# Feed-forward of a decoder trunk: plain token blocks copied beside the mixed ones, and four parts instead of three

## Chip, cores and metric

The kernel runs on one core of one Trainium2 chip. The time is device microseconds of one launch, from the first to the last thing that the core does; lower is better. A result is the median of several executions.

## What is computed

The reference is a trunk of two layers on 256 tokens of 2048 features, in fp32: a gated DeltaNet mixer, a SwiGLU feed-forward, an HGRN2 mixer, a second SwiGLU feed-forward, with an RMSNorm ahead of each and one at the end. The change touches the two feed-forwards alone:

```python
D_MODEL, SEQ = 2048, 256
D_FF = -(-8 * D_MODEL // (3 * 256)) * 256          # 5632
def swiglu(h, w_gate, w_up, w_down):
    return (jax.nn.silu(h @ w_gate) * (h @ w_up)) @ w_down
...
    h = h + swiglu(rmsnorm(h, ffn_norm[layer]), ffn_w_gate[layer], ffn_w_up[layer], ffn_w_down[layer])
```

## The kernel before, in words

**Products.** Every matrix product is made in fp32 precision from three products in a rounded format: a weight tile `raw` (128x1024, 512 KB) is loaded, ScalarE (ACT) rounds it to `wh`, VectorE (DVE) subtracts to get the rest `wl`, and TensorE (PE) adds token-high by `wh`, token-high by `wl` and token-low by `wh`. The tokens' halves `xt_h`, `xt_l` (four tiles each, 256 tokens by 4x128 features) live in a constant pool. In `mm_rows` (line 666) the token tile of 128x128 is the stationary operand and 512 weight columns move. One *item* is one 128x1024 weight tile: twelve products of 512 columns. Items are a list, made once in Python; `stream` (line 629) keeps the loads and splits three items ahead (`AHEAD`, line 35), with four buffers each for `raw`, `wh` and `wl`.

**Groups and pairs.** The 5632 hidden features are 22 groups of 256 gate and 256 up columns. A *plain* group (`gate_up`, line 914) is 8 items; its end applies SiLU on ACT (`sg`) and the product with `up` on DVE (`h`), in `gated` (line 873). Two groups make a pair. A pair's result has to be turned to be the stationary operand of the down product, `hth` and `htl`. `turned` (898) does that through DRAM (`turn_through`, 818): four transposes inside 32x32 blocks on DVE, one DMA out and four in, on the queue of GpSimd (POOL). The pairs of `FF_QUICK` (line 34), and these alone, are turned on DVE without DRAM, half a pair (one group) at a time, by sixteen small transposes (`turn`, 808, `turned_half`, 907).

**Strassen groups.** 8 of the 22 groups in each feed-forward (four pairs) are made by `mixed_group` (934): the tokens in two halves, the features in two halves and gate and up as the two column halves give seven block products instead of eight, each with 256 moving columns. A group is 16 items: four rounds of four. In a round, item 1 makes product 1, item 2 products 2 and 3, item 3 products 5 and 7, item 4 products 6 and 4. Items 1 and 2 load weights (`sraw`), the weights of items 3 and 4 are sums on DVE. Products 3, 5, 6, 7 have mixed tokens as stationary operand, made at the phase's start by `mix_inputs` (832) into two tiles, `mixh` and `mixl`, that start at bytes 108 and 364 of a partition modulo 512 (offset 19 words, padding `PAD`). Products 1, 2, 4 read plain tokens from `xt_h` and `xt_l`. The seven products lie in four PSUM banks of the pool `aux`; plain and down items use two tiles of the pool `main`. At a group's end (`end`, 1007) ACT copies products 1 and 4 out, DVE makes the sums, and `gated` follows.

**Order.** `among` (512) spreads the Strassen items evenly behind plain or down items, all but the last `tail` ones. `FF_PLAN` (26) is in pairs: pair 0 plain, pair 1 by Strassen among pairs 2 and 3; pair 4 by Strassen among the first down part, pair 7 among 5 and 6; pair 8 among the second down part, then pairs 9 and 10 plain, then the third down part alone. A down part (`down`, 1043) multiplies the pairs of its part by the down weights, in four column groups `cg`; each loads the residual `x` from DRAM, adds the product (`add_x`) and stores it back. The last part's column groups also make the next phase's tokens (`next_input`) or the final norm (`finish`). The items' order on PE is fixed by this list.

**Planner.** All operations are recorded, and `plan` (314) simulates the engines with a table of costs and puts each engine's instructions in an order: among those that are ready, the one with the earliest due time (`late`) goes first. A due time is counted back from the item that needs the result; the serial length of several operations on one engine is not in it. The chip then runs each engine's list in that order, whatever the real times are.

Of the kernel before, what the change touches and what calls it, by code (L numbers as in the profile page):

```python
# [8 lines left out]
F32 = mybir.dt.float32  # L9
F32R = mybir.dt.float32r  # L10
U8 = mybir.dt.uint8
AF = mybir.ActivationFunctionType
# [5 lines left out]
P = 128  # L18
T = 256
# [2 lines left out]
CH = 64  # L22
N_HG = 8
N_FF = 22
FF_PARTS = (8, 8, 6)
FF_PLAN = (
    "0 | 1:2,3",
    "4:down | 7:5,6",
    "8:down | 9 | 10",
)  # L30
N_HGRN = 4
LEVELS = (64, 32, 16, 8, 4, 2, 1)
MASKED = LEVELS[2:]
FF_QUICK = (3, 6, 10)
AHEAD = 3
RAW_BUFS = 4
SPLIT_BUFS = 4
# [42 lines left out]


PAD = 64
IN_COLS = {"wh": 108, "wl": 364}


# [435 lines left out]


class Trunk:
# [294 lines left out]
    def turn_through(self, out, x):  # L818

        blocks = self.tile(self.pool, [P, 4, T], "blocks", bufs=1)  # L820
# [6 lines left out]
        self.nc.gpsimd.dma_start(home, blocks)  # L827
        home = home.rearrange("(a f) b r -> b f a r", a=4)
        for b in range(4):
            self.nc.gpsimd.dma_start(out[32 * b : 32 * b + 32], home[b])  # L830

    def mix_inputs(self):
# [6 lines left out]
        self.mixed = [[], [], [], []]  # L839
        both = [self.tile(self.pool, [P, 4096 + PAD], f"mix{x}", F32R)[:, 19 : 19 + 4096] for x in "hl"]  # L840
        row = self.rstd_row.unsqueeze(1).broadcast_to([P, 4, T])
        for q in range(2):
            uv = []
            for cg in (q, 2 + q):
                t = self.tile(self.pool, [P, 4, T], "turned", bufs=2, ordered=True)
                tt(t, self.xt_h[cg].bitcast(F32), self.xt_l[cg].bitcast(F32), ALU.add)
                tt(t, t, row, ALU.mult)
                uv += [t[:, :, 0:P], t[:, :, P:T]]
            a11, a21, a12, a22 = uv
            sums = []  # L850
            for _ in range(2):
                t = self.tile(self.pool, [P, 2, 512], "h1", bufs=2, ordered=True)
                sums += [t[:, i, :].rearrange("p (k t) -> p k t", k=4) for i in range(2)]
            s1, s2, s3, s4 = sums
            tt(s1, a21, a22, ALU.subtract)
            tt(s2, a11, s1, ALU.subtract)
            tt(s3, a21, a11, ALU.subtract)
            tt(s4, a12, s2, ALU.subtract)
            for n in range(4):
                h, low = (  # L860
                    m[:, (2 * n + q) * 512 : (2 * n + q + 1) * 512].rearrange("p (k t) -> p k t", k=4)
                    for m in both
                )
                nc.scalar.activation(h, sums[n], AF.Copy)
                tt(low, sums[n], h.bitcast(F32), ALU.subtract)
                self.mixed[n].append((h, low))

    def ffn(self, j, after):
        nc, a = self.nc, self.a
        hts, h1s, quick = {}, {}, {}  # L870
        gu = a[f"ffn_gu{j}"]

        def gated(gi, tt, gate, up, col):
# [3 lines left out]
            out = h1s[gi // 2][:, tt, gi % 2 * T : (gi % 2 + 1) * T]  # L877
            sg = self.tile(self.pool, [P, T], "sg", bufs=2)
# [17 lines left out]
            )  # L896

        def turned(pair):
            t = self.tile(self.pool, [P, 4, T], "turned", bufs=2, ordered=True)
            self.turn_through(t, h1s[pair])  # L900
            places(pair)
            split(
                pair, t.rearrange("p a (m s) -> p m a s", s=32),
                lambda x: x.rearrange("p n (t a s) -> p (n t) a s", t=2, s=32),
            )

        def turned_half(gi):
            pair, half = divmod(gi, 2)
# [7 lines left out]
        def gate_up(gi):  # L916
            def end(ps):
                for tt in range(2):
                    gated(gi, tt, ps[:, tt, 0:T], ps[:, tt, T:512], self.rstd[:, tt : tt + 1])
                if gi // 2 in FF_QUICK:  # L920
                    turned_half(gi)
                elif gi % 2:
                    turned(gi // 2)
# [6 lines left out]
        def mixed_pair(pair):  # L930

            return mixed_group(2 * pair) + mixed_group(2 * pair + 1, lambda: turned(pair))

        def mixed_group(gi, then=None):

            banks, raws = [], {}
            tok = slice(0, P), slice(P, T)

            def plain(k0, tt):
                def operand(kt):  # L940
                    cg = k0 + kt // 4
                    return self.xt_h[cg][:, kt % 4, tok[tt]], self.xt_l[cg][:, kt % 4, tok[tt]]
                return operand

            def mixed(n):
                def operand(kt):
# [60 lines left out]
            def end():  # L1007
                t = lambda n, tag: self.tile(self.pool, [P, n], tag, ordered=True)
                first, last = self.rstd[:, 0:1], self.rstd[:, 1:2]
                p1, p4, v, c11 = t(T, "p1"), t(T, "p4"), t(T, "p6"), t(T, "p2")  # L1010
                both = t(2 * T, "p37").rearrange("p (h c) -> p h c", h=2)
                w = both[:, 0]
# [5 lines left out]
                nc.vector.tensor_tensor(out=v, in0=product(6), in1=p1, op=ALU.subtract)  # L1018
                nc.vector.tensor_tensor(out=p1, in0=product(5), in1=v, op=ALU.add)
                nc.vector.tensor_tensor(  # L1020
                    out=both, in0=banks[1].rearrange("p (h c) -> p h c", h=2),
                    in1=p1.unsqueeze(1).broadcast_to([P, 2, T]), op=ALU.add,
                )
                nc.vector.tensor_tensor(out=v, in0=product(7), in1=v, op=ALU.add)
                nc.vector.tensor_tensor(out=p4, in0=p4, in1=v, op=ALU.subtract)
                gated(gi, 0, c11, both[:, 0], None)
                gated(gi, 1, p4, both[:, 1], None)
                if then:
                    then()

            items = []
            for kk in range(4):
# [36 lines left out]

        items, waiting = [], None  # L1070
        for part, steps in enumerate(FF_PLAN):
            order = []
            for step in steps.split(" | "):
                mix, _, beside = step.partition(":")
                if not beside:
                    order.append(int(step))
                    items += gate_up(2 * order[-1]) + gate_up(2 * order[-1] + 1)
                    continue
                many = []
                if beside == "down":  # L1080
                    many, waiting = waiting, None
                else:
                    for p in beside.split(","):
                        order.append(int(p))
                        many += gate_up(2 * order[-1]) + gate_up(2 * order[-1] + 1)
                order.insert(-1 if beside != "down" else 0, int(mix))
# [774 lines left out]
    def finish(self, cg):  # L1861
        nc = self.nc
        if cg == 0:
            self.last = self.tile(self.pool, [P, 4096 + PAD], "mixl", F32R, ordered=True).bitcast(F32)[:, 0:D]
            nc.gpsimd.dma_start(self.last, self.a["final_norm"].broadcast_to([P, D]))
            self.y = self.tile(self.pool, [P, 4096 + PAD], "mixh", F32R, ordered=True).bitcast(F32)[:, 0:4096].rearrange("p (t c) -> p t c", t=2)
# [144 lines left out]
```

## Time and profile before

| | |
|---|---|
| median of 3 runs | 2739.97 us (2739.84 to 2740.65) |
| the profiled execution's own time | 2739.51 us |
| its span, first to last instruction | 2737.7 us |
| mean granted TensorE clock | 0.999 |
| PE, PE weight loads, DVE, ACT, POOL busy | 2719.8, 2355.8, 2168.5, 1549.2, 307.6 us |

All operations are issued from one helper line (L496), so rows are told apart by the tiles' names: `main<-wh,xt_h` is a product into PSUM `main` from the weights' high half and the tokens' high half. `PEld` is the weight load (the stationary operand), which overlaps PE. `x1664` is a count. A span of a matmul is modelled and longer than the time between two starts, so the spacing of starts is what tells the rate. In the chain of waits each row is a stretch of one cause. A bracket at a row's end is the engine's idle time before it, and who ended it.

### The profile page before, as it was taken

What the parts mean: (1) busy time and instruction counts of PE and PEld (TensorE: products, weight loads), DVE (VectorE), ACT (ScalarE), POOL (GpSimd) and SP (SyncE); (2) the same over time, 40 slices, a digit from 0 to 9 for tenths busy, and PEclk for the clock granted to TensorE, in tenths of its full rate; (3) what the DMA queues carried; (4) which work ended last, traced back from release to release, by engine and by line L of the source; (5) the groups of instructions that cost most, each with busy time, mean ns of one, the idle gap of its engine ahead of it and who ended that gap; (6) DMA issues with size and microseconds to landing.
All of it is one profiled execution on the core that took longest, in us unless ns stands there. A gap on an engine that the chain in (4) does not pass through costs nothing.

```text
span 2737.7 us, 44285 instructions
## 1 busy us (share of the span) xinstructions
PE 2719.8 (99%) x16822; PEld 2355.8 (86%) x16822; DVE 2168.5 (79%) x3309; ACT 1549.2 (57%) x2192; POOL 307.6 (11%) x466
## 2 busy tenths in 40 slices
PE   9999999999999999999999999999999999999998
PEld 9888888888888888888888989988888888888887
DVE  7787888877768898889867688778678898888665
ACT  6646666565555555555545556556465555555543
POOL 1213222232110000000010100000100000000000
PEclk9999999999999999999999999999999999999999
DMA  7686568686676667766676755545676667666764
GB/s 262 202 282 224 183 217 279 215 277 220 220 252 224 219 212 245 238 216 216 228 235 217 228 167 182 170 166 179 224 264 212 217 223 239 223 230 221 250 209 167
DMA packets 170376, 605.92 MB, mean 221 GB/s; under 512 B 21675, under 2 KB 22843, under 8 KB 170033
## 3 DMA queue, kind: packets, MB, share of 16 engines
q1 hardware_dynamic: 138912, 503.15, 56.1%
q0 software_dynamic: 30960, 99.08, 11.3%
q8 instruction: 132, 2.16, 0.3%
q14 instruction: 84, 0.68, 0.1%
q10 hardware_dynamic: 288, 0.85, 0.1%
HBM read 563.10 MB, written 39.89 MB: 220 GB/s over the span
## 4 chain that ended last, share of the span: by engine, by line
PE 96%; DVE 2%; ACT 1%; issue 1%; POOLq 0%; POOL 0%; DVEq 0%; ACTq 0%
PE main L496 80%; PE aux L496 17%; DVE wl L496 1%; DVE turned L496 1%; ACT wh L496 0%; ACT dec L496 0%; DVE htl L496 0%; DVE sraw L496 0%; ACT xt_h L496 0%; DVE h L496 0%; DVE utmp L496 0%; DVE pre L496 0%; DVE u L496 0%; ACT mixh L496 0%; POOLq L2007 0%
## 5 line engine op out<-in xcount | busy, mean ns | idle before, releaser
L496 ACT ACTIVATE wh<-raw 128x1024 fp32r<-128x1024 f32 x817 | 864.9, 1060 | 934.5 <-PE main L496 826.2
L496 DVE TENSOR_TENSOR wl<-raw,wh 128x1024 fp32r<-128x1024 f32 x817 | 1002.6, 1229 | 422.3 <-ACT wh L496 412.3
L496 PE MATMUL main<-wh,xt_h 128*128 128x512 f32 x1664 | 651.5, 391 | 0.8 <-ACT wh L496 0.8
L496 PE MATMUL main<-wl,xt_h 128*128 128x512 f32 x1664 | 650.7, 391 | 1.3 <-DVE wl L496 1.3
L496 PE MATMUL main<-wh,xt_l 128*128 128x512 f32 x1664 | 650.3, 391 | 0.0
L496 PEld LDWEIGHTS main<-wh,xt_l 128*128 128x128 f32 x1664 | 312.5, 188 | 65.1
L496 PEld LDWEIGHTS main<-wh,xt_h 128*128 128x128 f32 x1664 | 312.7, 188 | 62.8 <-ACT wh L496 1.2
L496 PEld LDWEIGHTS main<-wl,xt_h 128*128 128x128 f32 x1664 | 312.6, 188 | 61.7 <-DVE wl L496 1.6
L496 ACT ACTIVATE wh<-sraw 128x1024 fp32r<-128x1024 f32 (+1 forms) x256 | 243.4, 951 | 136.7 <-PE main L496 96.3
L496 DVE TENSOR_TENSOR wl<-sraw,wh 128x1024 fp32r<-128x1024 f32 (+1 forms) x256 | 278.3, 1087 | 27.1 <-ACT wh L496 25.0
L496 PE MATMUL main<-xt_h,wh 128*128 128x256 f32 (+1 forms) x1040 | 288.7, 278 | 0.7 <-ACT wh L496 0.7
L496 PE MATMUL main<-xt_h,wl 128*128 128x256 f32 (+1 forms) x1040 | 288.3, 277 | 1.1 <-DVE wl L496 0.9
L496 PE MATMUL main<-xt_l,wh 128*128 128x256 f32 (+1 forms) x1040 | 288.2, 277 | 0.3 <-DVE xt_l L496 0.3
L496 PE MATMUL main<-wh,hth 128*128 128x512 f32 x680 | 266.5, 392 | 1.0 <-ACT hth L496 1.0
L496 PE MATMUL main<-wl,hth 128*128 128x512 f32 x680 | 266.2, 391 | 0.0
L496 PE MATMUL main<-wh,htl 128*128 128x512 f32 x680 | 265.2, 390 | 0.4
L496 PEld LDWEIGHTS main<-xt_h,wl 128*128 128x128 f32 (+1 forms) x1040 | 194.4, 187 | 1.6 <-DVE wl L496 1.5
L496 PEld LDWEIGHTS main<-xt_h,wh 128*128 128x128 f32 (+1 forms) x1040 | 194.5, 187 | 1.3 <-ACT wh L496 0.9
L496 PEld LDWEIGHTS main<-xt_l,wh 128*128 128x128 f32 (+1 forms) x1040 | 194.5, 187 | 1.0 <-DVE xt_l L496 0.5
L496 PEld LDWEIGHTS main<-wh,htl 128*128 128x128 f32 x680 | 127.7, 188 | 29.2 <-DVE htl L496 1.7
L496 PE MATMUL main<-wh,ot_l 128*128 128x512 f32 x384 | 151.3, 394 | 0.0
L496 PE MATMUL main<-wh,ot_h 128*128 128x512 f32 x384 | 150.5, 392 | 0.0
(238 smaller groups left out, 4078.5 us busy)
## 6 DMA issues: line engine op xcount, KB each, us to landing
raw<-in_ffn_gu SPq DMA_DIRECT2D x224, 512.0 KB, 4.7
raw<-in_ffn_d SPq DMA_DIRECT2D x176, 512.0 KB, 4.7
sraw<-in_ffn_gu SPq DMA_DIRECT2D x128, 512.0 KB, 5.2
raw<-in_hgrn_in SPq DMA_DIRECT2D x128, 512.0 KB, 4.1
raw<-in_gdn_kq SPq DMA_DIRECT2D x64, 512.0 KB, 5.3
raw<-in_gdn_v SPq DMA_DIRECT2D x64, 512.0 KB, 4.8
raw<-in_gdn_z SPq DMA_DIRECT2D x64, 512.0 KB, 4.9
raw<-in_gdn_out SPq DMA_DIRECT2D x64, 512.0 KB, 5.1
```

The source lines that it names most:

```text
L496: getattr(getattr(tc.nc, op.eng), op.method)(*args, **kw)
```

## The change

1. `mix_inputs` makes two more blocks in `mixh` and `mixl` (6 instead of 4 blocks of 1024 columns): copies, on ACT, of the plain tokens of products 2 and 4. Product 1 still reads `xt_h` and `xt_l`.
2. Four parts of 6, 6, 6, 4 groups instead of three of 8, 8, 6. The plan is now in groups; each part starts with one plain group, and the down part before it follows that group. There are still 8 Strassen groups in each feed-forward: 2, then 6, 7, 9, then 12, 13, 15, then 18. `among` has a `head` of plain items ahead of the first Strassen item besides the `tail`.
3. Only pair 10 is still turned on DVE; pairs 3 and 6 now go through DRAM as the others do. `blocks` shares the two buffers of `turned`.
4. The end of a Strassen group works in place, with fewer buffers: ACT no longer copies product 4, DVE reads it from PSUM as its last step; product 6 is read before product 2.

The diff, cut to its core:

```diff
-FF_PARTS = (8, 8, 6)
+FF_PARTS = (6, 6, 6, 4)
 FF_PLAN = (
-    "0 | 1:2,3",
-    "4:down | 7:5,6",
-    "8:down | 9 | 10",
+    "0 | 2 : 1 3 4 5 : 6 2",
+    "6 7 9 : 8 down 10 11 : 4 4",
+    "12 13 15 : 14 down 16 17 : 4 4",
+    "18 : 19 down 20 21 : 4 12",
 )
-FF_QUICK = (3, 6, 10)
+FF_QUICK = (10,)
+MIXED = 6 * 1024
...
-def among(few, many, tail):
+def among(few, many, head, tail):
...
-        upto = min(len(few), -(-len(few) * (i + 1) // (len(many) - tail)))
+        upto = max(0, min(len(few), -(-len(few) * (i + 1 - head) // (len(many) - head - tail))))
...
-            for n in range(4):
+            for n in range(6):
...
-                nc.scalar.activation(h, sums[n], AF.Copy)
-                tt(low, sums[n], h.bitcast(F32), ALU.subtract)
+                if n < 4:
+                    nc.scalar.activation(h, sums[n], AF.Copy)
+                    tt(low, sums[n], h.bitcast(F32), ALU.subtract)
+                else:
+                    cg, half = ((2 + q, 0), (2 + q, 1))[n - 4]
+                    t = slice(half * P, (half + 1) * P)
+                    nc.scalar.activation(h, self.xt_h[cg][:, :, t].bitcast(F32), AF.Copy)
+                    nc.scalar.activation(low, self.xt_l[cg][:, :, t].bitcast(F32), AF.Copy)
...
             uses = {
-                1: (plain(0, 0), 0, 0), 2: (plain(2, 0), 0, 1), 3: (mixed(4), 1, 0), 7: (mixed(3), 1, 1),
-                5: (mixed(1), 2, 0), 6: (mixed(2), 2, 1), 4: (plain(2, 1), 3, 0),
+                1: (plain, 0, 0), 2: (mixed(5), 0, 1), 3: (mixed(4), 1, 0), 7: (mixed(3), 1, 1),
+                5: (mixed(1), 2, 0), 6: (mixed(2), 2, 1), 4: (mixed(6), 3, 0),
             }
...
                 nc.scalar.activation(p1, product(1), AF.Copy, scale=first)
-                nc.scalar.activation(p4, product(4), AF.Copy, scale=last)
+                nc.vector.tensor_tensor(out=v, in0=product(6), in1=p1, op=ALU.subtract)
                 nc.vector.scalar_tensor_tensor(
-                    out=c11, in0=product(2), scalar=first, in1=p1, op0=ALU.mult, op1=ALU.add
+                    out=p1, in0=product(2), scalar=first, in1=p1, op0=ALU.mult, op1=ALU.add
                 )
...
                 nc.vector.tensor_tensor(out=v, in0=product(7), in1=v, op=ALU.add)
-                nc.vector.tensor_tensor(out=p4, in0=p4, in1=v, op=ALU.subtract)
+                nc.vector.scalar_tensor_tensor(
+                    out=v, in0=product(4), scalar=last, in1=v, op0=ALU.mult, op1=ALU.subtract
+                )
...
-                items += among(mixed_pair(int(mix)), many, 2 if beside == "down" else 6)
+                items += among([i for g in few.split() for i in mixed_group(int(g))], many, *spare)
             assert waiting is None
+            lo = sum(FF_PARTS[:part]) // 2
+            order = range(lo, lo + FF_PARTS[part] // 2)
             waiting = [i for cg in range(4) for i in down(part, cg, order)]
```

More of the change, by code (lines that the diff above doesn't have):

```diff
@@ L816, in turn, with turn_through @@
                 )
-    def turn_through(self, out, x):
-        blocks = self.tile(self.pool, [P, 4, T], "blocks", bufs=1)
+    def turn_through(self, x):
+        blocks = self.tile(self.pool, [P, 4, T], "turned", bufs=2, ordered=True)
         home = self.tile(self.dram, [P, 4, T], "blocks_home")
@@ L827, in turn_through @@
         self.nc.gpsimd.dma_start(home, blocks)
+        out = self.tile(self.pool, [P, 4, T], "turned", bufs=2, ordered=True)
         home = home.rearrange("(a f) b r -> b f a r", a=4)
@@ L830, in turn_through @@
             self.nc.gpsimd.dma_start(out[32 * b : 32 * b + 32], home[b])
+        return out
     def mix_inputs(self):
@@ L837, in tt @@
             nc.vector.tensor_tensor(out=out, in0=a, in1=b, op=op)
-        self.mixed = [[], [], [], []]
-        both = [self.tile(self.pool, [P, 4096 + PAD], f"mix{x}", F32R)[:, 19 : 19 + 4096] for x in "hl"]
+        self.mixed = [[] for _ in range(6)]
+        both = [self.tile(self.pool, [P, MIXED + PAD], f"mix{x}", F32R)[:, 19 : 19 + MIXED] for x in "hl"]
         row = self.rstd_row.unsqueeze(1).broadcast_to([P, 4, T])
@@ L898, in turned @@
         def turned(pair):
-            t = self.tile(self.pool, [P, 4, T], "turned", bufs=2, ordered=True)
-            self.turn_through(t, h1s[pair])
+            t = self.turn_through(h1s[pair])
             places(pair)
@@ L905, in turned, with finished @@
             )
+        def finished(gi):
+            done.add(gi)
+            if gi ^ 1 in done:
+                turned(gi // 2)
         def turned_half(gi):
@@ L921, in end @@
                     turned_half(gi)
-                elif gi % 2:
-                    turned(gi // 2)
+                else:
+                    finished(gi)
             return self.group(
@@ L928, in gate_up, with mixed_group, plain @@
             )
-        def mixed_pair(pair):
-            return mixed_group(2 * pair) + mixed_group(2 * pair + 1, lambda: turned(pair))
-        def mixed_group(gi, then=None):
+        def mixed_group(gi):
             banks, raws = [], {}
[L937 to L943, printed above, removed]
+            def plain(kt):
+                return tuple(x[:, 0:P] for x in self.operand(kt))
             def mixed(n):
@@ L1071, in ffn @@
         for part, steps in enumerate(FF_PLAN):
-            order = []
             for step in steps.split(" | "):
[L1074 to L1077, printed above, removed]
+                few, _, rest = step.partition(" : ")
+                if not rest:
+                    items += gate_up(int(step))
                     continue
+                beside, tail = rest.split(" : ")
                 many = []
[L1080 to L1086, printed above, removed]
-                items += among(mixed_pair(int(mix)), many, 2 if beside == "down" else 6)
+                for g in beside.split():
+                    if g == "down":
+                        many, waiting = many + waiting, None
+                    else:
+                        many += gate_up(int(g))
+                spare = (int(n) for n in tail.split())
+                items += among([i for g in few.split() for i in mixed_group(int(g))], many, *spare)
             assert waiting is None
+            lo = sum(FF_PARTS[:part]) // 2
+            order = range(lo, lo + FF_PARTS[part] // 2)
             waiting = [i for cg in range(4) for i in down(part, cg, order)]
@@ L1863, in finish @@
         if cg == 0:
-            self.last = self.tile(self.pool, [P, 4096 + PAD], "mixl", F32R, ordered=True).bitcast(F32)[:, 0:D]
+            self.last = self.tile(self.pool, [P, MIXED + PAD], "mixl", F32R, ordered=True).bitcast(F32)[:, 0:D]
             nc.gpsimd.dma_start(self.last, self.a["final_norm"].broadcast_to([P, D]))
-            self.y = self.tile(self.pool, [P, 4096 + PAD], "mixh", F32R, ordered=True).bitcast(F32)[:, 0:4096].rearrange("p (t c) -> p t c", t=2)
+            self.y = self.tile(self.pool, [P, MIXED + PAD], "mixh", F32R, ordered=True).bitcast(F32)[:, 0:4096].rearrange("p (t c) -> p t c", t=2)
             self.part = self.tile(self.pool, [P, 2], "part")
```

28 lines of the change are left out of this document (14 added, 14 removed).

## The prediction

> **What bounds the kernel now.** I read the page first (busy shares, chain of waits), then the windows of the first feed-forward, then the chain and the timeline inside it.
>
> ```profile
> span 2737.7 us, 44285 instructions
> PE 2719.8 (99%) x16822; PEld 2355.8 (86%) x16822; DVE 2168.5 (79%) x3309; ACT 1549.2 (57%) x2192; POOL 307.6 (11%) x466
> ```
> ```profile
> 827.00:872.00 45.00, 45.00 (x208) 37.49 (x207) 41.40 (x54) 24.24 (x36) 2.00 (x3) 1.00 0.65 224
> 872.00:980.00 108.00, 108.00 (x637) 95.65 (x636) 94.68 (x117) 63.36 (x73) 5.54 (x10) 1.00 0.67 220
> 980.00:1024.00 44.00, 44.00 (x232) 37.82 (x231) 40.98 (x73) 22.53 (x27) 2.74 (x5) 1.00 0.69 214
> ```
>
> A windows row gives the stretch, its length, then the busy time of PE, weight loads, DVE, ACT, POOL, the granted clock (1.00) and the DMA share. PE is never idle in these three stretches, from the start of the first feed-forward to the start of its first down part. DVE is the second engine: 94.68 of 108 us (88%) where Strassen and plain items alternate, 40.98 of 44 (93%) just after. So time can come from two places only: PE's own spacing of matmuls, and the few places where PE waits. Both feed-forwards hold the same 112 plain, 88 down and 128 Strassen items before and after. I counted the stretches of Strassen items between plain ones, too: 112 per feed-forward in both lists. What it costs to change between the kinds is therefore unchanged.
>
> **Term 1: the stationary operand's place.** The chain of waits, window 826 to 1000, gives the last three items of a round of a Strassen group, each behind a plain item (start, us, what). The timeline shows starts inside item 2 (first two rows; `xt`) and inside item 3 (last two; `mix`).
>
> ```profile
> 914.60 1.41 PE aux L496 x12
> 916.01 2.74 PE main L496 x12
> 918.76 1.38 PE aux L496 x12
> 920.13 2.75 PE main L496 x12
> 922.88 1.42 PE aux L496 x12
> ```
> ```profile
> 915.14 0.28 PE L496 MATMUL aux<-wh,xt_h 128*128 128x256 f32 x1
> 915.26 0.28 PE L496 MATMUL aux<-wl,xt_h 128*128 128x256 f32 x1
> ...
> 919.06 0.28 PE L496 MATMUL aux<-wl,mixh 128*128 128x256 f32 x1
> 919.17 0.28 PE L496 MATMUL aux<-wh,mixl 128*128 128x256 f32 x1
> ```
>
> With plain tokens as stationary operand these matmuls of 256 columns start 0.12 us apart, with mixed ones 0.11. Item 3, all mixed, takes 1.38 us; items 2 and 4, half plain, 1.41 and 1.42. After the change items 2 and 4 have stationary operands from the same two tiles as item 3, so I give them its 1.38: 0.03 + 0.04 = 0.07 us a round. There are 8 groups x 4 rounds x 2 feed-forwards = 64 rounds: 4.5 us. At best all 768 matmuls of products 2 and 4 (64 rounds x 12) gain the 0.01 us between the two spacings, 7.7 us; at worst the place isn't the cause and it is 0. I take **-4.8**, near the items' rows, a little more for the 16 stretches per feed-forward in which two Strassen items follow each other.
>
> The Trainium skill, "SBUF — State Buffer", section "Who interferes with whom", speaks against this term: TensorE has an independent read port for the weight load, and "PE and ACT never wait on anyone". By that, one place of the stationary operand should be as good as another, and term 1 would be 0. The two spacings above don't bear that out, though they don't show that bytes are the cause either; this is the first rival.
>
> **Term 2: the junctions.** A down part whose last pair was turned by small transposes makes PE wait. First the PE timeline at 1024, then DVE's beside it, then the weight loads' groups over the whole span.
>
> ```profile
> 1024.76 0.28 PE L496 MATMUL aux<-wh,xt_l 128*128 128x256 f32 x1
> 1025.29 0.50 PE L496 MATMUL main<-wh,hth 128*128 128x512 f32 x1 [0.25 <-ACT hth L496]
> 1025.63 0.42 PE L496 MATMUL main<-wl,hth 128*128 128x512 f32 x1
> 1026.14 0.50 PE L496 MATMUL main<-wh,htl 128*128 128x512 f32 x1
> 1026.48 0.40 PE L496 MATMUL main<-wh,hth 128*128 128x512 f32 x1
> ```
> ```profile
> 1019.19 5.04 DVE L496 STREAM_TRANSPOSE turned<-h 32x128 f32<-32x128 f32 x16
> ...
> 1025.41 0.68 DVE L496 TENSOR_TENSOR htl<-turned,hth 128x512 fp32r<-128x512 f32 x1
> ```
> ```profile
> L496 PEld LDWEIGHTS main<-wh,hth 128*128 128x128 f32 x680 | 127.9, 188 | 24.8 <-ACT hth L496 1.8
> L496 PEld LDWEIGHTS main<-wh,htl 128*128 128x128 f32 x680 | 127.7, 188 | 29.2 <-DVE htl L496 1.7
> ```
>
> From 1024.76 to 1026.48 are 1.72 us; one spacing of 0.12 and three of 0.227 (2.72 us an item over 12) would be 0.80. So 0.92 us is lost, behind sixteen transposes in a row. Two such junctions in each feed-forward make 3.7 us, and the groups' waits of 1.8 and 1.7 us bear that out. After the change pairs 3 and 6 go through DRAM, and each down part is behind a plain group: its last pair is needed 12 plain items, over 33 us, after it was made. What takes the place of the transposes is late next, but not late: four transposes, a store, four loads and the split by the rows below. **-3.7**, bounds 0 and -3.7.
>
> ```profile
> L496 DVE STREAM_TRANSPOSE blocks<-h 128x256 f32<-128x256 f32 x64 | 25.2, 425 | 0.2
> L496 DVE TENSOR_TENSOR x<-x,main 128x1024 f32<-128x1024 f32 x47 | 57.3, 1220 | 17.5 <-PE main L496 17.2
> L496 ACT ACTIVATE mixh<-h 128x512 fp32r<-128x512 f32 x16 | 9.5, 619 | 1.3 <-DVE h L496 1.3
> ```
> ```profile
> DMA to landing us min/median/max: 2.8/5.6/9.1
> ```
>
> The landing row is that of the tile `blocks_home`: 4 x 0.425 for the transposes, 5.6 for the store, 5.6 for the loads, 1.06 and 1.23 as for a weight tile's split (rows below) make 15 us; at the slowest landing, 9.1 twice, 22, still under 33.
>
> **Term 3: the last junction.** Pair 10 keeps its small transposes. Before, the last part has three pairs, so PE has four items of other pairs before pair 10 and a fifth for its first half. Now it has two and one: the second half is needed 3 x 2.72 = 8.2 us after the last plain matmul instead of 13.6. The timeline of the last junction, PE, ACT, DVE:
>
> ```profile
> 2662.01 0.39 PE L496 MATMUL main<-wh,xt_l 128*128 128x512 f32 x1
> 2662.24 0.39 PE L496 MATMUL main<-wh,hth 128*128 128x512 f32 x1
> ```
> ```profile
> 2662.49 1.06 ACT L496 ACTIVATE wh<-raw 128x1024 fp32r<-128x1024 f32 x1 [1.66 <-PE main L496]
> 2663.45 0.82 ACT L496 ACTIVATE sg<-main,rstd 128x256 f32<-128x256 f32 x2
> ```
> ```profile
> 2664.72 0.87 DVE L496 SCALAR_TENSOR_TENSOR h<-main,rstd,sg 128x256 f32<-128x256 f32 x2
> 2665.63 0.30 DVE L496 STREAM_TRANSPOSE turned<-h 32x128 f32<-32x128 f32 x1
> 2666.25 1.23 DVE L496 TENSOR_TENSOR wl<-raw,wh 128x1024 fp32r<-128x1024 f32 x1 [0.32 <-ACT wh L496]
> 2667.51 4.74 DVE L496 STREAM_TRANSPOSE turned<-h 32x128 f32<-32x128 f32 x15
> 2672.29 1.23 DVE L496 TENSOR_TENSOR wl<-raw,wh 128x1024 fp32r<-128x1024 f32 x1
> 2673.43 0.68 DVE L496 TENSOR_TENSOR htl<-turned,hth 128x512 fp32r<-128x512 f32 x1
> ```
>
> In this order `htl` is ready at 2674.1. The new list wants it at 2662.24 + 8.17 + 0.45 = 2670.9: 3.2 us late, some 3.5 with the slow restart. But the order won't stay: the planner goes by due time, and the chain is now due 5.4 us earlier. `sg` ahead of the `wh` at 2662.49 saves 1.0, transposes ahead of the `wl` at 2666.25 another 1.2, and of the 1.1 of the `wl` at 2672.29 a part, since `htl` needs `hth` from ACT first. The end is then 2670.8 to 2671.9, in time or 1 us late. Between 0 and 3.5 us per feed-forward I take 0.6, near the due-time order: **+1.2** in all, bounds 0 and +7.
>
> **Costed at nothing.** DVE loses 128 small transposes (4 pairs; 5.04 us per 16) and gains 16 of 0.425 and 8 `x` sums of 1.22: some 23 us less. In the long stretches (40 slots, 48 Strassen items) I scale the stretch from 872 to 980, which has 25 plain and 32 Strassen items: DVE needs (94.68 - 25 x 1.14) x 1.5 + 40 x 1.14 + 4 x 1.22 = 150 us, PE (108 - 25 x 2.75) x 1.5 + 40 x 2.75 = 169: 89%, where it was 88% (1.14 is the time from the `wl` at 2672.29 to the operation behind it). ACT's 16 copies of 0.62 go into 24.24 of 45 us, but the first Strassen item comes two plain items (5.5 us) earlier while DVE is at 41.40 of 45; without that cover perhaps 1 us each. POOL's 36 more DMAs (per feed-forward 8 for `x`, 5 for each of two pairs) sit on an engine 11% busy. The `x` load of column group 2 in the last part has 3 x 4 x 2.72 = 33 us where it had 3 x 6 x 2.72 = 49, for a sum, a store and a load. SP's weight loads only change order with the items. The end's new order lets DVE wait for product 6 before product 2's bank is free; behind it in DVE's queue stand the next splits:
>
> ```profile
> 923.98 0.42 DVE L496 TENSOR_TENSOR p<-aux,p 128x256 f32<-128x256 f32 x1 [0.47 <-PE aux L496]
> ```
>
> Item 4 of the chain's row at 922.88 ends at 924.30, and a plain item of 2.75 us stands ahead of the next group: from 923.98 that is 3.1 us, which hides two more DVE operations of 0.42 and a split of 1.23.
>
> **Sum.** -4.8 - 3.7 + 1.2 = -7.3 us. On the profiled execution (2739.51, of which 2737.7 are span) 2732.2; on the median of 2739.97, 0.5 above it, **2732.7**.
>
> **Rivals.**
> - *The place is not the cause* (0.12): the slower spacing comes from the items' order or weights, or the copies don't land where the title says. Then -3.7 + 1.2: 2737.5. For it: no row ties the spacing to bytes. Against: items 2 to 4 have the same tiles of `wh` and `wl` and the same shapes, and differ in the stationary operand alone.
> - *The last junction keeps its order* (0.11): -8.5 + 7 = -1.5, 2738.5. For it: due times don't count serial transposes, which is how the old junctions came to wait.
> - *Small waits* (0.11) at eight group boundaries or at the earlier Strassen starts, some 4 us: 2736.7.
> - *DVE becomes the bound* (0.06), slower than before: three Strassen groups run together for 169 us, four times. At 89% it doesn't; if clustering (three group ends, four sums) takes its need past PE's 169 us, by 3% say, PE waits 5 us a stretch, 20 in all: -8.5 + 20, 2751. It decides from 100% of DVE on; 93% stands beside the old waits.
> - Forecast: 0.60.
>
> About 0.2% (5.5 us) is what a measurement of this kernel can tell from no change. Faster by more: 0.63 (the forecast and a little of the small waits); within: 0.31; slower: 0.06. The range 2730.0 to 2738.0 goes from both terms at their best, less an error of the median, to the first rival, and leaves the slower one and part of the last-junction rival out.
>
> **What would show it.** Right: items 2 and 4 at 1.37 to 1.38 in the chain and `aux<-wh,xt_h` down from three products' 64 x 2 to one's 128; no idle weight loads before `hth` at the first three junctions; at the last one `sg` ahead of `wh`. Wrong: items still 1.41; a PE wait of over 2 us some 8 us after the last plain group; DVE over 95% in the long stretches.

## The result, and the profile after

| | before | after |
|---|---|---|
| median (range, 8 runs each) | 2740.31 us (2739.34 to 2741.46) | 2731.73 us (2731.23 to 2733.75) |
| ratio, 95% interval | | 0.997 (0.9959 to 0.9981) |
| profiled execution; its span | 2739.51; 2737.7 | 2733.75; 2732.0 |
| first mixer, until its last product starts | 823.72 | 826.18 |
| first feed-forward | 710.14 | 706.06 |
| second mixer | 486.03 | 486.03 |
| second feed-forward | 707.40 | 703.35 |
| behind it | 10.41 | 10.41 |

The change saves 8.6 us, 0.31%; by the interval 5.2 to 11.2. The profiled execution of after is the slowest of its eight: its first mixer, which the change doesn't touch, took 2.5 us longer, and this is not the change's: a run below, with the change in it, has 823.85 there. A stage here is the time between two starts on PE, from the last product of one stage to the last product of the next. All of the gain lies in the two feed-forwards, 4.08 and 4.05 us.

The page of after, its span and engines:

```profile
span 2732.0 us, 44265 instructions
PE 2714.4 (99%) x16822; PEld 2351.4 (86%) x16822; DVE 2150.6 (79%) x3201; ACT 1548.8 (57%) x2188; POOL 332.7 (12%) x502
```

The same 16822 matmuls are there, PE is the bound as before, and DVE has 108 instructions fewer. The helper's line is now L498. Next the windows of after, from the start of the first feed-forward over two of the stretches in which three Strassen groups run together (columns as in the prediction):

```profile
826.00:867.00 41.00, 41.00 (x189) 34.10 (x188) 37.47 (x47) 25.38 (x38) 3.69 (x3) 1.00 0.74 250
867.00:953.00 86.00, 86.00 (x462) 74.25 (x461) 68.82 (x82) 46.22 (x53) 2.79 (x5) 1.00 0.65 208
953.00:1130.00 177.00, 177.00 (x1017) 155.43 (x1016) 150.61 (x181) 96.74 (x108) 14.06 (x23) 1.00 0.74 242
1130.00:1300.00 170.00, 170.00 (x967) 148.92 (x967) 144.15 (x175) 91.15 (x101) 11.29 (x18) 1.00 0.72 237
```

PE's busy time equals the stretch in each row, so it doesn't wait here beyond what the modelled spans hide (0.39 us for a product of 512 columns, with starts 0.227 apart). The starts on PE themselves are nowhere more than 0.09 us late from 826 to 1300. DVE is at 91% of the first 41 us, and at 85% in the two long stretches. The chain of waits of after has the first round's items 2, 3 and 4 (`aux`, 12 products each) behind plain ones:

```profile
872.18 1.38 PE aux L498 x12
873.55 5.46 PE main L498 x24
879.02 1.38 PE aux L498 x12
880.39 2.74 PE main L498 x12
883.14 1.38 PE aux L498 x12
```

Items 2 and 4, which took 1.41 and 1.42 us, now take 1.38 like item 3. The groups of PE and of its weight loads show who still reads plain tokens, and who is waited for:

```profile
L498 PE MATMUL aux<-wh,xt_h 128*128 128x256 f32 x128 | 35.9, 280 | 0.0
...
L498 PEld LDWEIGHTS main<-wh,hth 128*128 128x128 f32 x688 | 129.3, 188 | 23.7
L498 PEld LDWEIGHTS main<-wl,hth 128*128 128x128 f32 x688 | 129.3, 188 | 22.8 <-DVE wl L498 0.4
L498 PEld LDWEIGHTS main<-wh,htl 128*128 128x128 f32 x688 | 129.2, 188 | 28.5 <-DVE htl L498 0.8
```

Product 1 alone reads `xt_h` in the Strassen groups (x128). The wait for `hth` (1.8 us before) has no releaser any more, and that for `htl` is down from 1.7 to 0.8 us, 0.4 per feed-forward. That rest is the last junction. Its timeline in the second feed-forward, ACT, then DVE, then PE:

```profile
2678.03 0.84 ACT L498 ACTIVATE sg<-main,rstd 128x256 f32<-128x256 f32 x2 [1.61 <-PE main L498]
2678.76 1.06 ACT L498 ACTIVATE wh<-raw 128x1024 fp32r<-128x1024 f32 x1
...
2684.89 0.63 ACT L498 ACTIVATE hth<-turned 128x512 fp32r<-128x512 f32 x1 [0.37 <-DVE turned L498]
```
```profile
2678.90 0.87 DVE L498 SCALAR_TENSOR_TENSOR h<-main,rstd,sg 128x256 f32<-128x256 f32 x2 [1.23 <-ACT sg L498]
2679.81 5.05 DVE L498 STREAM_TRANSPOSE turned<-h 32x128 f32<-32x128 f32 x16
2684.89 1.23 DVE L498 TENSOR_TENSOR wl<-raw,wh 128x1024 fp32r<-128x1024 f32 x1
2686.03 0.68 DVE L498 TENSOR_TENSOR htl<-turned,hth 128x512 fp32r<-128x512 f32 x1
```
```profile
2685.99 0.39 PE L498 MATMUL main<-wh,hth 128*128 128x512 f32 x1
2686.21 0.46 PE L498 MATMUL main<-wl,hth 128*128 128x512 f32 x1
2686.77 0.50 PE L498 MATMUL main<-wh,htl 128*128 128x512 f32 x1
2687.11 0.40 PE L498 MATMUL main<-wh,hth 128*128 128x512 f32 x1
```

ACT does `sg` ahead of the next `wh`, DVE all sixteen transposes ahead of the next `wl`. This one `wl` still stands ahead of `htl`, though `hth` is done at 2685.52, and the third product starts 0.56 instead of 0.227 us behind the second, the fourth 0.34 behind the third: 0.45 us lost per feed-forward.

### The profile page after: what moved, and what is told of

It reads as the page before. It is cut to its first block, busy times and chain, and to the rows that moved or that the text cites. A ratio compares the mean times of both kernels' runs of the same rounds, so it can differ in the third digit from the quotient of the medians.

```text
span 2732.0 us, 44265 instructions
## 1 busy us (share of the span) xinstructions
PE 2714.4 (99%) x16822; PEld 2351.4 (86%) x16822; DVE 2150.6 (79%) x3201; ACT 1548.8 (57%) x2188; POOL 332.7 (12%) x502
## 4 chain that ended last, share of the span: by engine, by line
PE 97%; DVE 1%; DMA 1%; issue 0%; ACT 0%; SPq 0%; POOLq 0%; POOL 0%; DVEq 0%; ACTq 0%
PE main L498 80%; PE aux L498 17%; DVE turned L498 0%; DVE wl L498 0%; DMA raw<-in_gdn_z 0%; DMA first<-in_x 0%; ACT dec L498 0%; ACT wh L498 0%; DVE h L498 0%; DVE htl L498 0%; DVE utmp L498 0%; DVE pre L498 0%; SPq L498 0%; ACT xt_h L498 0%; DVE u L498 0%
## 5 line engine op out<-in xcount | busy, mean ns | idle before, releaser
L498 ACT ACTIVATE wh<-raw 128x1024 fp32r<-128x1024 f32 x817 | 863.9, 1060 | 838.2 <-PE main L498 688.8
L498 DVE TENSOR_TENSOR wl<-raw,wh 128x1024 fp32r<-128x1024 f32 x817 | 1000.7, 1227 | 359.5 <-ACT wh L498 347.5
L498 PE MATMUL main<-wh,xt_h 128*128 128x512 f32 x1664 | 651.4, 391 | 0.8 <-ACT wh L498 0.8
L498 PE MATMUL main<-wl,xt_h 128*128 128x512 f32 x1664 | 650.7, 391 | 1.3 <-DVE wl L498 1.3
L498 PE MATMUL main<-wh,xt_l 128*128 128x512 f32 x1664 | 650.2, 391 | 0.0
L498 ACT ACTIVATE wh<-sraw 128x1024 fp32r<-128x1024 f32 (+1 forms) x256 | 243.8, 952 | 229.3 <-PE main L498 189.4
L498 PEld LDWEIGHTS main<-wh,xt_l 128*128 128x128 f32 x1664 | 312.5, 188 | 65.4
L498 PEld LDWEIGHTS main<-wh,xt_h 128*128 128x128 f32 x1664 | 312.5, 188 | 62.7 <-ACT wh L498 1.2
L498 PEld LDWEIGHTS main<-wl,xt_h 128*128 128x128 f32 x1664 | 312.4, 188 | 61.7 <-DVE wl L498 1.6
L498 DVE TENSOR_TENSOR wl<-sraw,wh 128x1024 fp32r<-128x1024 f32 (+1 forms) x256 | 278.5, 1088 | 101.8 <-ACT wh L498 99.7
L498 PE MATMUL main<-xt_h,wh 128*128 128x256 f32 (+1 forms) x1040 | 289.4, 278 | 0.7 <-ACT wh L498 0.7
L498 PE MATMUL main<-xt_h,wl 128*128 128x256 f32 (+1 forms) x1040 | 288.7, 278 | 0.9 <-DVE wl L498 0.9
L498 PE MATMUL main<-xt_l,wh 128*128 128x256 f32 (+1 forms) x1040 | 288.5, 277 | 0.3 <-DVE xt_l L498 0.3
L498 PE MATMUL main<-wl,hth 128*128 128x512 f32 x688 | 269.4, 392 | 0.0
L498 PE MATMUL main<-wh,hth 128*128 128x512 f32 x688 | 269.2, 391 | 0.0
L498 PE MATMUL main<-wh,htl 128*128 128x512 f32 x688 | 268.0, 390 | 0.2
L498 PE MATMUL aux<-wh,mixl 128*128 128x256 f32 x768 | 213.0, 277 | 0.0
L498 PE MATMUL aux<-wl,mixh 128*128 128x256 f32 x768 | 212.8, 277 | 0.0
L498 PE MATMUL aux<-wh,mixh 128*128 128x256 f32 x768 | 212.8, 277 | 0.0
L498 PEld LDWEIGHTS main<-xt_h,wh 128*128 128x128 f32 (+1 forms) x1040 | 194.8, 187 | 1.3 <-ACT wh L498 0.9
L498 PEld LDWEIGHTS main<-xt_h,wl 128*128 128x128 f32 (+1 forms) x1040 | 194.7, 187 | 1.2 <-DVE wl L498 1.1
L498 PEld LDWEIGHTS main<-xt_l,wh 128*128 128x128 f32 (+1 forms) x1040 | 194.7, 187 | 1.0 <-DVE xt_l L498 0.5
```

Source lines behind the costliest of these rows:

```text
L498: getattr(getattr(tc.nc, op.eng), op.method)(*args, **kw)
```

## The experiments

The theory is that of the prediction: the gain is the place of the stationary operand (some 5 us) plus the junctions (some 3.7), less the last junction (some 1). The rivals: that not the place but the order or the extra tile brings the first part, and that the way of turning, not the later start of a down part, brings the second.

### The copies: is it the place?

**Copies made, but not read** (after, with products 2 and 4 reading `xt_h` and `xt_l` again):

```diff
-                1: (plain, 0, 0), 2: (mixed(5), 0, 1), 3: (mixed(4), 1, 0), 7: (mixed(3), 1, 1),
-                5: (mixed(1), 2, 0), 6: (mixed(2), 2, 1), 4: (mixed(6), 3, 0),
+                1: (plain(0, 0), 0, 0), 2: (plain(2, 0), 0, 1), 3: (mixed(4), 1, 0), 7: (mixed(3), 1, 1),
+                5: (mixed(1), 2, 0), 6: (mixed(2), 2, 1), 4: (plain(2, 1), 3, 0),
```

> The changed kernel, but products 2 and 4 read the plain tokens from xt_h and xt_l again (the copies are still made, and not read). Theory (the place of the stationary operand sets the spacing): items 2 and 4 back at 1.41 and 1.42 us, each feed-forward 2.3 to 2.6 us longer, 2731.7 + 5 = about 2737. Rival (the spacing belongs to the list of items): items 2 and 4 stay at 1.38, 2731.7.

Measured: 2737.57 us (2736.82 to 2738.81), ratio 0.9991 (0.9982 to 1.0). Its feed-forwards take 708.76 and 706.02 us, that is 2.70 and 2.67 more than after's, a little over the expected 2.3 to 2.6. The chain has the old items again:

```profile
870.71 1.41 PE aux L498 x12
872.12 5.46 PE main L498 x24
877.58 1.38 PE aux L498 x12
878.96 2.74 PE main L498 x12
881.70 1.42 PE aux L498 x12
```

So reading from the copies is worth 5.4 us, with the order, the weights and the copying itself unchanged.

**The same tiles from their first word**, bytes 32 and 288 instead of 108 and 364:

```diff
-        both = [self.tile(self.pool, [P, MIXED + PAD], f"mix{x}", F32R)[:, 19 : 19 + MIXED] for x in "hl"]
+        both = [self.tile(self.pool, [P, MIXED + PAD], f"mix{x}", F32R)[:, 0:MIXED] for x in "hl"]
```

> The changed kernel with the two tiles of mixed and copied tokens used from their first word on, so that they start at bytes 32 and 288 modulo 512 instead of 108 and 364. Theory (the bytes count): the stationary operands of items 2, 3 and 4 are then where the plain tokens are (32), and all three items take 1.41 us or more: 64 rounds x 3 x 0.03 to 0.05 us = 6 to 10 us, 2738 to 2742. Rival (a tile of its own counts, wherever it starts): 1.38 us, 2731.7.

Measured: 2744.53 us (2743.47 to 2745.62), ratio 1.0015 (1.0006 to 1.0025): 12.8 us more than after by 76 bytes alone. Every Strassen item of twelve products now takes 1.43 us, the all-mixed one too. A tile of its own brings nothing; the bytes do. The size was more than expected: as means over the traces an item went from 1.374 to 1.432 us, 0.058 more, where 0.03 to 0.05 was allowed.

**The moving weights at 108 and 364 too** (the copies unread, as in the first run; weights of row items start where the mixed tokens do):

```diff
-            want = IN_COLS[v.tag] if v.cols else 32 + n % 2 * 512
+            want = IN_COLS[v.tag]
```

> As e1_plain24 (products 1, 2, 4 read plain tokens at byte 32, the four others mixed tokens at 108 and 364), but the moving weights of all items start at 108 (high) and 364 (low) instead of 32. Theory A: the same as e1_plain24, 2737.6, items 2, 3, 4 at 1.41, 1.38, 1.42. Theory B: the plain products become fast and the mixed ones slow, item 1 under 0.70 and item 3 over 1.40 us, the whole 2737 to 2743.

Measured: 2747.14 us (2746.3 to 2748.44), ratio 1.0024 (1.0014 to 1.0033). The chain, items 3 and 4:

```profile
880.10 1.43 PE aux L498 x12
881.53 2.74 PE main L498 x12
884.27 1.41 PE aux L498 x12
```

The all-mixed item, whose two operands now start at the same bytes, went from 1.38 to 1.43, what byte 32 against byte 32 costs. Item 1, all plain, went the other way, from 0.71 to 0.70 us. So theory A falls: the place of the stationary operand isn't good or bad by itself; it is so in relation to the moving one. B had the direction but not the size: item 1 isn't under 0.70, and the whole is 4 us over its range. I took from it that equal start bytes are what is slow.

**Four other places for the same two tiles** put that to the test. Each is after with the same line edited, and the 19 replaced by 1 (bytes 36 and 292), 16 (96 and 352), 32 (160 and 416) or 51 (236 and 492); for the first:

```diff
-        both = [self.tile(self.pool, [P, MIXED + PAD], f"mix{x}", F32R)[:, 19 : 19 + MIXED] for x in "hl"]
+        both = [self.tile(self.pool, [P, MIXED + PAD], f"mix{x}", F32R)[:, 1 : 1 + MIXED] for x in "hl"]
```

> The change with its two tiles of mixed and copied tokens started one word on: bytes 36 and 292 modulo 512 instead of 108 and 364. The moving weights start at byte 32. Theory A (only equal start bytes, modulo 256, make a 256-column product slow): every Strassen product with these tiles is spaced 113 ns, each feed-forward takes 703 to 706 us, in all about 2732. Rival B (what counts is the 64-byte or 32-byte piece in which both start): bytes 32 and 36 lie in one piece, so 120 ns as at byte 32, each feed-forward 709 to 712 us, in all about 2744.5. Between the two (some 116 ns, 2738) would speak for a cost that falls with the distance.

> The same two tiles at bytes 96 and 352 modulo 512, that is 64 bytes on from the place of the moving weights at 32. Theory A (only equal start bytes modulo 256 are slow): 113 ns, about 2732. Rival C (what counts is the start modulo 64, or a smaller power of two, such as alignment to 32 bytes): 96 and 32 are alike modulo 64, so 120 ns and about 2744.5.

> The same two tiles at bytes 160 and 416 modulo 512, that is 128 bytes on from the place of the moving weights at 32. Theory A (only equal start bytes modulo 256 are slow): 113 ns, about 2732. Rival C (modulo 128, 64 or 32): 120 ns, about 2744.5. If 96 is fast and 160 slow, the period is 128.

> The change with its two tiles of mixed and copied tokens 128 bytes further on: bytes 236 and 492 modulo 512 instead of 108 and 364. Starts at 32, 36, 96 and 160 gave 1.43, 1.41, 1.42 and 1.45 us for an all-mixed Strassen item, 108 gives 1.38. Theory D (what counts is the start modulo 128, so 236 is as good as 108): 1.38 us an item, feed-forwards of 706 and 703 us, about 2732. Rival E (the period is 256 or longer, as 32 and 160, which are alike modulo 128, already differ by 0.02 us an item): 1.40 to 1.45 us an item, 2738 to 2748.

Measured (the item is the first round's all-mixed one, from the chain of each run; the moving weights start at 32 in all):

| `mixh` and `mixl` start at (modulo 512) | item, us | feed-forwards, us | median, us | ratio to before |
|---|---|---|---|---|
| 32, 288 | 1.43 | 712.09, 709.33 | 2744.53 | 1.0015 (1.0006 to 1.0025) |
| 36, 292 | 1.41 | 710.65, 707.90 | 2742.02 | 1.0001 (0.999 to 1.0012) |
| 96, 352 | 1.42 | 710.08, 707.31 | 2740.12 | 0.9998 (0.9986 to 1.0009) |
| 108, 364 | 1.38 | 706.06, 703.35 | 2731.73 | 0.997 (0.9959 to 0.9981) |
| 160, 416 | 1.45 | 714.49, 711.75 | 2748.49 | 1.003 (1.0014 to 1.0046) |
| 236, 492 | 1.47 | 716.41, 713.67 | 2752.30 | 1.0044 (1.0024 to 1.0064) |

By these rows 36 looks faster than 96; as means over the 144 such items of a trace the two are alike, 1.412 and 1.413 us. The chain's rows of bytes 160 and 236, one fence each:

```profile
879.05 1.45 PE aux L498 x12
```
```profile
878.56 1.47 PE aux L498 x12
```

All four theories A to D fall. Different start bytes aren't enough for the short item (36, 96, 160). A common piece of 32 or 64 bytes isn't the whole cost, as 36 is faster than 32. A period of 64 would make 32, 96 and 160 alike, and their first feed-forwards take 712.1, 710.1 and 714.5 us. A period of 128 would make 236 like 108, and one is the slowest, the other the fastest. Rival E to the period foresaw the failure but not its size, 1.47 instead of at most 1.45. What is shown: by the place of two tiles alone the same program differs by up to 20.6 us. By which rule stays open.

**No copies: the tokens themselves at 108 and 364** (after's plan; `xt_h` and `xt_l` become views of two large tiles, the mixed tiles have four blocks):

```diff
-        self.xt_h = [t([P, 4, T], f"xt_h{i}", F32R) for i in range(4)]
-        self.xt_l = [t([P, 4, T], f"xt_l{i}", F32R) for i in range(4)]
+        xt = [t([P, 4096 + PAD], f"xt_{x}", F32R)[:, 19 : 19 + 4096] for x in "hl"]
```

> The changed plan, without the two copied blocks: instead the plain tokens themselves, xt_h and xt_l, start at bytes 108 and 364 modulo 512. For the Strassen items both theories give 1.38 us or less, and item 1 (product 1) gains too, 0.71 to 0.69: 64 x 0.02 = 1.2 us. In the column items of the mixers the plain tokens are the moving operand, and the weights, at 108 and 364, the stationary one. Theory A (a stationary operand that starts at byte 32 is slow by itself): they don't change, the HGRN2 phase stays at 486.0 us, the whole 2730.5. Theory B (slow is a stationary operand whose bytes modulo 512 are those of the moving one): they become slow, 0.120 for 0.113 us at 1536 matmuls in the HGRN2 phase and as many in the first mixer, 486 + 10, the whole about 2751.

Measured: 2780.49 us (2780.16 to 2780.55), ratio 1.0144 (1.0128 to 1.016). Both theories missed the whole: neither had the products of 512 columns in it. The Strassen items came about as expected (means of 1.38 us, item 1 0.70). The first plain items of after, and of this run, in the chain:

```profile
866.00 2.72 PE main L498 x12
```
```profile
865.90 21.23 PE main L498 x91
```

After spaces products of 512 columns by 2.72 / 12 = 0.227 us, this run by 21.23 / 91 = 0.233. The place that suits 256 moving columns costs 512 of them 3%. The second mixer is longer by 14.5 us (486.03 to 500.50). Added up from the starts on PE, its 1536 column products, with these tokens as the moving operand, take 9.9 us more (0.120 instead of 0.114 us each), which is theory B's 10. Its 768 products of 512 columns with these tokens as the stationary operand take 4.5 us more.

**The same, with the mixers' weights at 32 and 288** instead of 108 and 364:

```diff
-IN_COLS = {"wh": 108, "wl": 364}
+IN_COLS = {"wh": 32, "wl": 288}
```

> As e3_xt108, and the weights of column items moved from bytes 108 and 364 to 32 and 288, so that there the stationary operand is at 32 and 288 and the moving one at 108 and 364. Theory A (byte 32 is slow for a stationary operand): column items slow, HGRN2 phase 486 + 10 us, the whole about 2751. Theory B (equal bytes are slow): column items as before, 486, the whole 2730.5.

Measured: 2771.03 us (2769.75 to 2771.16), ratio 1.0108 (1.009 to 1.0126). The second mixer takes 495.48 us, a third of the way back, and the feed-forwards stay (713.55 and 710.87). The column products come half of the way back, to 0.117 us each; the products of 512 columns don't change. Swapping the two operands' places doesn't restore the old spacing. That is a second sign that equal bytes aren't the whole rule.

### The junctions: the way of turning, or the later start?

**Before, with pairs 3 and 6 through DRAM**, nothing else:

```diff
-FF_QUICK = (3, 6, 10)
+FF_QUICK = (10,)
```

> The kernel before, three parts as they were, but pairs 3 and 6 turned through DRAM as well. Theory (the sixteen small transposes in DVE's queue are what makes PE wait): the trip through DRAM, some 22 us, just fits into the 25 us that these pairs have, and the waits at the two junctions go: 2740.3 - 3.7 = 2736.6. Rival (what matters is that a down part begins a group later): the trip comes late, 5 us or more at each of four junctions instead of 0.92: 2756 or more.

Measured: 2764.43 us (2761.88 to 2766.18), ratio 1.009 (1.0075 to 1.0105). The theory failed and the rival was right: the trip doesn't fit. DVE's last `h` of the pair at the first junction, POOL's queue, and then PE:

```profile
1000.76 0.87 DVE L496 SCALAR_TENSOR_TENSOR h<-main,rstd,sg 128x256 f32<-128x256 f32 x2
```
```profile
1009.69 0.56 POOL L496 DMA_DIRECT2D blocks_home<-blocks  x1 [5.06 <-DVE blocks L496]
1015.03 2.18 POOL L496 DMA_DIRECT2D turned<-blocks_home  x4 [4.79 <-DMA blocks_home<-blocks]
```
```profile
1023.09 0.28 PE L496 MATMUL aux<-wh,mixl 128*128 128x256 f32 x1
1025.08 0.50 PE L496 MATMUL main<-wh,hth 128*128 128x512 f32 x1 [1.72 <-ACT hth L496]
1025.41 0.40 PE L496 MATMUL main<-wl,hth 128*128 128x512 f32 x1
1028.12 0.50 PE L496 MATMUL main<-wh,htl 128*128 128x512 f32 x1 [2.31 <-DVE htl L496]
1028.46 0.43 PE L496 MATMUL main<-wh,hth 128*128 128x512 f32 x1
1028.69 0.63 PE L496 MATMUL main<-wl,hth 128*128 128x512 f32 x1
1029.12 0.63 PE L496 MATMUL main<-wh,htl 128*128 128x512 f32 x1
```

The store is issued at 1009.69 and the loads at 1015.03; PE wants the pair at 1023.2 and gets `hth` at 1025.1 and `htl` at 1028.1, 18 us after the store and 26 after the last `h`. On top of the wait comes a second price, in the windows of this run:

```profile
1029.00:1031.60 2.60, 2.60 (x7) 1.99 (x7) 0.00 (x0) 0.00 (x0) 0.00 (x0) 0.50 0.07 24
1031.60:1040.00 8.40, 8.40 (x47) 7.25 (x46) 5.95 (x6) 4.21 (x5) 0.72 (x1) 0.97 0.44 156
```

Behind the two waits the granted clock is 0.50, and a product of 512 columns takes 0.43 us instead of 0.227 for some 3 us. The feed-forwards are 12.5 and 11.7 us longer than before's.

**After, with every part's last pair turned on DVE**:

```diff
-FF_QUICK = (10,)
+FF_QUICK = (2, 5, 8, 10)
```

> The changed kernel, but pairs 2, 5 and 8, the last of their parts, turned by small transposes on DVE as pairs 3 and 6 were. Theory (a down part that begins a group later leaves time enough for either way): no wait at the junctions, 2731.7. Rival (sixteen transposes in a row hold up the splits wherever they stand): 0.9 us at each of six junctions, 2737.

Measured: 2731.39 us (2731.13 to 2731.87), ratio 0.9969 (0.9958 to 0.9981), the same as after; the first mixer takes 823.85 us in its trace, the feed-forwards 706.05 and 703.32. Its long stretches in the windows:

```profile
953.00:1130.00 177.00, 177.00 (x1021) 155.56 (x1020) 157.61 (x203) 97.36 (x108) 11.32 (x18) 1.00 0.71 234
1130.00:1300.00 170.00, 170.00 (x966) 148.86 (x965) 151.40 (x200) 90.37 (x101) 9.12 (x14) 1.00 0.71 234
```

DVE is at 89% instead of 85%, and PE waits for nothing. With the down part one plain group later, either way of turning is in time; without that, the trip through DRAM costs 24 us. So it is the new list, in which the down part starts later, that removed the waits. That the later start does it alone, without the four parts, is likely but wasn't run. The trip only unloads DVE, which isn't the bound.

### The last junction

**Parts of 6, 6, 4 and 6 groups**, so that the last part has three pairs again:

```diff
-FF_PARTS = (6, 6, 6, 4)
+FF_PARTS = (6, 6, 4, 6)
...
-    "12 13 15 : 14 down 16 17 : 4 4",
-    "18 : 19 down 20 21 : 4 12",
+    "12 13 : 14 down 15 : 4 4",
+    "16 18 : 17 down 19 20 21 : 4 12",
```

> The changed kernel with parts of 6, 6, 4, 6 groups (Strassen groups 2; 6, 7, 9; 12, 13; 16, 18), so that the last part has three pairs and pair 10, turned by small transposes, is needed two items later. Theory (the last junction waits because its second half is needed 8.2 us after the last plain matmul): the wait of about 0.45 us in each feed-forward goes, 2731.7 - 0.9 = 2730.8. Rival (DVE's work in the last part is what is late): the wait stays, or grows, as the last part has more Strassen items ahead: 2731.7 or more.

Measured: 2731.93 us (2730.59 to 2732.79), ratio 0.9968 (0.9955 to 0.998). The 0.45 us between `wl` and `htl` is gone at both last junctions, and the feed-forwards take 705.89 and 703.14 us, 0.17 and 0.21 less than after's. Of the expected 0.9 only 0.38 came, and a median can't show it. The rest probably went to the list: it has 120 stretches of Strassen items per feed-forward instead of 112, and a plain item behind a stretch takes 2.74 to 2.75 us in after's chain instead of 2.72. Eight times 0.03 is an estimate of 0.2 us. None of the runs beats after by more than the spread.

## Why the prediction was right

**Sum.** Forecast -7.3 us, measured -8.6 by the medians and -8.1 by the feed-forwards of the two traces.

**Term 1, the place: -4.8 forecast, -5.4 measured** (copies unread against after). The mechanism is shown: the place, not the order, the weights or the tile. The size came from rows rounded to 0.01 us, and that it is so near is partly luck. As means over the traces, items 2 and 4 lost 0.032 and 0.046 us, not 0.03 and 0.04. That makes 5.0 us in 64 rounds, and the stretches of two items in a row add some 0.2.

The upper bound of 7.7 took 0.01 us a product. The two spacings are 0.120 and 0.113 us, and 768 times their difference is 5.1. Nor were the plain products alone slow: in before's half-plain items three mixed products behind plain ones took 0.118, 0.118 and 0.113. PE's timeline in after's first item 2, the first, fourth and seventh products:

```profile
872.02 0.28 PE L498 MATMUL aux<-wh,mixh 128*128 128x256 f32 x1
...
872.37 0.28 PE L498 MATMUL aux<-wh,mixh 128*128 128x256 f32 x1
...
872.71 0.28 PE L498 MATMUL aux<-wh,mixh 128*128 128x256 f32 x1
```

From the first to the fourth start are 0.35 us, from the fourth to the seventh 0.34: 0.118 and 0.113 apiece, as means over the 144 items of twelve products that stand alone between plain ones. So the first three behind a plain item stay slower even in after.

The Trainium skill, "SBUF — State Buffer", section "Who interferes with whom", would have made this term 0, with its independent port for the weight load. The runs decide against it as far as time goes: the same program at other bytes costs 12.8 us (byte 32) and 20.6 us (byte 236) more. Whether a port is what is fought over, no run shows.

**Term 2, the junctions: -3.7 forecast, -3.8 measured.** Added up from the starts in before's PE trace, its four junctions lose 0.92, 0.96, 0.96 and 0.93 us, where I had read 0.92. After loses nothing at the first three junctions of either feed-forward. With the place and the 0.9 given back this makes 8.3 us, against 8.1 by the feed-forwards; no more than that is left for the new end of the Strassen groups, which no run tests alone. Of the two reasons given, the trip through DRAM and the plain group ahead, the first doesn't do it: with it alone the kernel lost 24 us.

The trip itself was mis-sized, without harm. I had 15 to 22 us from the transposes to `htl`, as if each step began when the last one ended. At after's first junction (DVE, then PE's first product with the pair):

```profile
958.80 0.87 DVE L498 SCALAR_TENSOR_TENSOR h<-main,rstd,sg 128x256 f32<-128x256 f32 x2
...
969.63 1.42 DVE L498 STREAM_TRANSPOSE turned<-h 128x256 f32<-128x256 f32 x4
...
994.37 1.22 DVE L498 TENSOR_TENSOR htl<-turned,hth 128x1024 fp32r<-128x1024 f32 x1
```
```profile
1000.88 0.40 PE L498 MATMUL main<-wh,hth 128*128 128x512 f32 x1
```

The transposes began 10 us after the last `h`, and `htl` was done at 995.6, 36 us after it and 26 after the transposes' start. That is more than the 33 us that I had counted on. It was in time because Strassen items stand between the plain ones, so that the pair is needed 41 us after the last `h`.

**Term 3, the last junction: +1.2 forecast, +0.9 measured**, in the order that was forecast: `sg` ahead of `wh`, the transposes ahead of `wl`. That the `wl` ahead of `htl` would stay in part was foreseen as well, and it is the whole of the loss: without it `htl` could have started when `hth` was done, 0.5 us earlier.

**Costed at nothing.** DVE: 89% forecast for the long stretches, 85% found. The first Strassen item at 91% of DVE cost no wait; the windows show no PE idle there. The second mixer's length, 486.03 us on both sides, shows that nothing was pushed out of the first feed-forward into it.

**The rivals.** That the place is not the cause falls by the unread copies and by byte 32. The last junction did change its order. Small waits would stand among PE's starts: of both feed-forwards of after, none outside the last down parts is more than 0.09 us late. DVE as the bound stays away even at the 89% of the run with every pair turned on DVE.

## What to carry to other kernels

When products of one shape show two spacings in the timeline, compare the tiles' start bytes before anything else: copying an operand to another place, or only starting its tile some words later, may be worth more than a change of order. Find the place by trying it in the whole kernel: the best one here held for 256 moving columns and one place of the moving operand, and was a loss for 512. At a junction between stages, first ask whether the consumer can start one group later; that removed the waits here with either way of turning, where taking the turning off DVE alone made them longer.

## What the runs showed of the hardware that was not expected

- Start bytes matter finely: 1.38 to 1.47 us for twelve products of 256 columns, with 4 bytes (32 to 36) worth 2.5 us of the kernel and 128 bytes (108 to 236) 20.6 us. Neither 128 bytes nor a smaller power of two fits as a period. The cause is open.
- The same place helps one shape and harms another: with the tokens at 108 and 364 products of 512 columns went from 0.227 to 0.233 us.
- Two waits of 1.72 and 2.31 us, with 0.7 us of work between them, were followed by some 3 us at half the granted clock. The Trainium skill, "TensorE: Matmul & The Clock Gate", section "What's actually happening", gives half rate after an idle window of about 3.4 us; the halving agrees, though neither wait alone was that long.
